# FFN up projection of a decoder trunk: x's hi and x's lo stored side by side and multiplied by the weights' hi in one matmul of 512 columns, with eight PSUM banks as one pool in the FFNs

## The chip, the cores and the metric

The kernel runs on one core of a Trainium2 chip. The metric is the device time of one execution in microseconds (us); smaller is better.

## The reference

Two post-norm layers on an input of 256 tokens by 2048 channels, all in float32. Each layer is a mixer and a feed-forward network (FFN) with a short causal convolution, each with a residual and a layer norm (LN). The part that the change touches is the FFN:

```python
D_MODEL = 2048; SEQ = 256; DEPTH = 2; D_FF = 5632; FFN_CONV = 3
# every layer: x <- LN(alpha*x + mixer(x)); x <- LN(alpha*x + conv_ffn(x))
# conv_ffn: u = x @ w_up                     (2048 -> 2*5632: gate half, value half)
#           u = causal depthwise conv of 3 taps over the tokens
#           y = (silu(gate) * value) @ w_down  (5632 -> 2048)
```

## The kernel before

**Three-term products.** Every float32 operand of a large matmul is split into hi (rounded to the type that TensorE multiplies) and lo (the rest). A product is three matmuls that add into one PSUM tile: hi·hi, hi·lo and lo·hi. Weights come as 1 MB blocks of 512 rows by 512 columns (`load_w`: DMA into `raw`, ACT makes `hi` at L127, DVE makes `lo` at L128). Eight `hi` and eight `lo` buffers let the loads run ahead of TensorE. x lies transposed, channels on partitions, in tiles `XH` (hi) and `XL` (lo), stored as [partition, token half t, channel tile k, 128 tokens]. The 256 tokens of one channel tile are therefore two pieces of 128 with a gap between them.

**Three kinds of projection.** `proj_a` holds weights still and streams the 256 tokens: per channel tile kt and output tile ct it issues L145 (hi·XH), L146 (hi·XL) and L147 (lo·XH), 256 columns each. `proj_b` holds x still and streams 512 weight columns (L178, L179, L181). `proj_halves` does the same for one token half after the other (L213 to L215); the last two column blocks of each output projection run in it, so that the LN of half t=0 can begin while half t=1 is still being multiplied. `proj_bt` is a `proj_b` whose result is transposed afterwards. It makes the first block after an LN, because it can work on half t=0 before half t=1 exists.

**Stages.** `run` goes through even mixer, FFN 0, odd mixer, FFN 1. An FFN has 11 pairs. A pair is a gate block (`proj_bt` in pair 0, `proj_a` in the others) and a value block (`proj_a`), each followed by the convolution (`conv`: ACT L312, DVE L313 and L314 per output tile), and a part of the down projection. During pairs 2 to 9 of FFN 0 a block `s5_prep_block` each is put in, which prepares tables for the odd mixer: eight transposes (L700), eight small matmuls (L709, sixteen instructions in the trace), a DVE copy and a DVE add (L711, L715), and one matmul on their result (L717).

**LN.** `layer_norm(t)`: bn_aggr and L257 on DVE, a power on POOL (L258), four DVE operations L260, four L266, then per column block four transposes on TensorE (L274), an ACT copy to `XH` (L277) and a DVE subtraction to `XL` (L278).

**PSUM.** Eight banks: a pool `acc` of four tiles (one bank each) and a pool `ps` of four, for the whole program. `proj_a` takes two `acc` tiles, `ps` serves transposes and the small matmuls of the stages.

**Order.** The instructions of each engine are put into one fixed order when the program is built, by a scheduler that takes buffers and dependences into account. An engine carries out its instructions in that order, and an instruction that waits holds all that stand behind it on its engine.

Of the kernel before, what the change touches and what calls it, by code (L numbers as in the profile page):

```python
# [7 lines left out]
F32 = mybir.dt.float32  # L8
F32R = mybir.dt.float32r
AF = mybir.ActivationFunctionType  # L10
ALU = mybir.AluOpType
AX = mybir.AxisListType
PSUM = bass.MemoryType.PSUM
DRAM = bass.MemoryType.DRAM

P = 128
T = 256
D = 2048
KT = D // P
DFF = 5632  # L20
# [8 lines left out]
ALL = slice(None)  # L29
# [32 lines left out]
class Build:  # L62
    def __init__(self, ctx, tc, I, O, cols):
        self.tc, self.nc, self.I, self.O = tc, tc.nc, I, O
        self.cols = cols
        nc = self.nc
        self.nld, self.alternate = 0, False
        ctx.enter_context(nc.allow_non_contiguous_dma(reason="strided weight blocks"))
        pool = lambda n, b, **k: ctx.enter_context(tc.tile_pool(name=n, bufs=b, **k))
        self.cp = pool("cp", 1)  # L70
        self.rawp = pool("rawp", 3)
        self.hip = pool("hip", 8)
        self.lop = pool("lop", 8)
        self.sm = pool("sm", 2)
        self.W = self.cp.tile([P, NW, 2, 512], F32, name="W")
        self.accp = pool("accp", 4, space=PSUM)
        self.psp = pool("psp", 4, space=PSUM)
        self.drp = pool("drp", 1, space=DRAM)
        self.Xd = self.drp.tile([T, D], F32, name="Xd")
        self.XHt = [self.cp.tile([P, 2, 8, P], F32R, name=f"XH{k}") for k in range(2)]  # L80
        self.XLt = [self.cp.tile([P, 2, 8, P], F32R, name=f"XL{k}") for k in range(2)]
        ncst = sum(w for _, w in cols[0].values())
        cst = self.cp.tile([P, ncst], F32, name="cst")
        self.cst = cst
        g = lambda n: cst[:, cols[0][n][0]:cols[0][n][0] + cols[0][n][1]]
        self.ident, self.ones = g("ident"), g("ones")
        col = g("col")
        self.eps6, self.one, self.mhalf = (col[:, k:k + 1] for k in range(3))

    def xh(self, t, k, n=None):  # L90
        return self.XHt[k // 8][:, t, k % 8, :] if n is None else self.XHt[k // 8][:, t, k % 8:k % 8 + n, :]

    def xl(self, t, k, n=None):
        return self.XLt[k // 8][:, t, k % 8, :] if n is None else self.XLt[k // 8][:, t, k % 8:k % 8 + n, :]

    def ps(self):
        return self.psp.tile([P, 512], F32, name="ps")

    def acc(self):
        return self.accp.tile([P, 512], F32, name="acc")  # L100
# [30 lines left out]
    def proj_a(self, src, c0, epi, n=512, nkt=KT, pre=None):  # L131
        nc = self.nc
        nct = n // P
        accs = [self.acc() for _ in range((nct + 1) // 2)]
        for kg in range(nkt // 4):
            if pre and kg:
                pre(4 * kg, 4)
            w = self.load_w(src, kg * 512, c0, n, pre=pre if kg == 0 else None)
            for k in range(4):
                kt = kg * 4 + k  # L140
                xh, xl = self.xh(ALL, kt), self.xl(ALL, kt)
                for ct in range(nct):
                    a = accs[ct // 2][:, (ct % 2) * T:(ct % 2) * T + T]
                    wh, wl = (x[:, ct * P:ct * P + P] for x in w(k))
                    nc.tensor.matmul(a, wh, xh, start=kt == 0 and ct % 2 == 0, stop=False, skip_group_check=True)  # L145
                    nc.tensor.matmul(a, wh, xl, start=False, stop=False, skip_group_check=True)  # L146
                    nc.tensor.matmul(a, wl, xh, start=False, stop=kt == nkt - 1, skip_group_check=True)  # L147
        epi(accs)

    def proj_bt(self, src, c0, epi, buf, n=512, skip=0, side=None, tok_outer=True):  # L150
        nc = self.nc
# [148 lines left out]
    def conv_ffn(self, l, final, bg=None):  # L300
        nc, I = self.nc, self.I
        cw = self.wk.tile([P, 88, 3], F32, name="fcw")
        nc.sync.dma_start(cw, I["fcw"][l])
        up, down = I["ffn_w_up"][l], I["ffn_w_down"][l]
        hs = {}

        def conv(accs, ct0, dst):
            for ct in range(4):
                a = accs[ct // 2][:, (ct % 2) * T:(ct % 2) * T + T]
                w = lambda k: cw[:, ct0 + ct, k:k + 1]  # L310
                o = dst[:, ct, :]
                nc.scalar.activation(o, a, AF.Identity, scale=w(2))  # L312
                nc.vector.scalar_tensor_tensor(o[:, 1:], a[:, :T - 1], w(1), o[:, 1:], op0=ALU.mult, op1=ALU.add)  # L313
                nc.vector.scalar_tensor_tensor(o[:, 2:], a[:, :T - 2], w(0), o[:, 2:], op0=ALU.mult, op1=ALU.add)  # L314

        def pair(p):
            gt = self.w4k(4 + p % 2)

            def eg(accs):
                conv(accs, p * 4, gt)  # L320
                nc.scalar.activation(gt, gt, AF.Silu)

            def ev(accs):
                vt = self.w4k(6 + p % 2)
                conv(accs, 44 + p * 4, vt)
                nc.vector.tensor_tensor(vt, vt, gt, op=ALU.mult)
                hh = self.wk.tile([P, 4, T], F32R, name="hh", bufs=2)
                hl = self.wk.tile([P, 4, T], F32R, name="hl", bufs=2)
                nc.scalar.activation(hh, vt, AF.Copy)
                nc.vector.tensor_tensor(hl, vt, hh.bitcast(F32), op=ALU.subtract)  # L330
                hs[p] = (hh, hl)

            if p == 0:
                self.proj_bt(up, 0, eg, self.w4(8))
            else:
                self.proj_a(up, p * 512, eg)
            self.proj_a(up, DFF + p * 512, ev)

        def down_part(ps, last=None):
            lhs = lambda kt, t: tuple(h[:, kt % 4, t * P:t * P + P] for h in hs[ps[kt // 4]])  # L340
            self.out_add(down, ps[0] * 512, 4 * len(ps), lhs, ps[0] == 0, last)

        for p in range(NFF):
            pair(p)
            if bg and p in bg:
                bg[p]()
            if 0 < p < NFF - 1:
                down_part([p - 1])
        self.ln_params(I["ln_ffn_g"], I["ln_ffn_b"], l, (9, 10, 11, 12))
        down_part([NFF - 2, NFF - 1], lambda t: self.layer_norm(t, final, not final))  # L350
# [15 lines left out]
    def even_mixer(self):  # L366
# [91 lines left out]
        for t in range(2):  # L458
            ps = self.ps()
            for j in range(4):  # L460
                nc.tensor.transpose(ps[:, j * P:j * P + P], kd[:, j, t * P:t * P + P], self.ident)
            nc.scalar.copy(kdT[:, t, :], ps)
# [634 lines left out]
                                    op=ALU.subtract)  # L1097
            self.proj_a(self.I["glu_w"], ci * 512, eg, nkt=8)

    def dump(self, name):  # L1100
        nc = self.nc
        for which in ("XH", "XL"):
            n = f"{name}_{which}"
            if n in self.O:
                for k in range(2):
                    nc.sync.dma_start(self.O[n].rearrange("p (t k c) -> p t k c", t=2, k=16)[:, :, 8 * k:8 * k + 8],
                                      getattr(self, which + "t")[k].bitcast(F32))
        if f"{name}_X" in self.O:
            for cc in range(4):
                nc.sync.dma_start(self.O[f"{name}_X"].rearrange("p (t d) -> p t d", t=2)[:, :, cc * 512:cc * 512 + 512], self.X[cc])  # L1110

    def run(self, upto=4):
        nc = self.nc
        self.st = {}
        if upto >= 1:
            with self.phase("wk0", True):
                self.even_mixer()
            self.dump("m0")
        if upto >= 2:
            bg = {1: self.s5_prep_small}  # L1120
            for b in range(8):
                bg[b + 2] = lambda b=b: self.s5_prep_block(b)
            with self.phase("wk1"):
                self.conv_ffn(0, False, bg)
            self.dump("f0")
        if upto >= 3:
            with self.phase("wk2", True):
                self.odd_mixer()
            self.dump("m1")
        if upto >= 4:  # L1130
            with self.phase("wk3"):
                self.conv_ffn(1, True)

    @contextmanager
    def phase(self, name, mixer=False):
        with self.tc.tile_pool(name=name, bufs=1) as wk:
            self.wk = wk
            if mixer:
                self.W2 = wk.tile([P, 4, 2, 512], F32, name="W2")
            yield  # L1140
# [56 lines left out]
```

## Time and profile before

| | |
|---|---|
| median of 3 runs (lowest to highest) | 2462.37 us (2460.4 to 2462.51) |
| profiled execution, its own time | 2460.67 us |
| span in its profile | 2458.8 us, so 1.9 us lie outside |
| TensorE (PE) busy | 2424.9 us, 99% of the span |
| DVE, ACT, POOL busy | 1524.7, 1105.8, 638.8 us |
| granted TensorE clock, mean | 0.991 of full speed (2.4 GHz) |

The profiled execution is 1.7 us below the median of the runs. In the profile, L12 is line 12 of the kernel, PE is TensorE and PEld its weight load. A busy PE is one whose pipeline is not empty: a single row gives the time from a matmul's start to its modelled end (0.28 us for 256 columns), and in a dense stream the next one starts earlier.

### The profile page before, as it was taken

The page shows a single profiled execution, that of the slowest core. Times are in us where ns is not written, and L with a number is a line of the kernel's source. Part 1 is how long each engine was busy: PE and PEld are TensorE (multiplying, and loading weights), DVE is VectorE, ACT ScalarE, POOL GpSimd, SP SyncE. Part 2 cuts the span into 40 slices and gives each one's busy share as a digit, 9 for nine tenths or more (in the row PEclk, how much of TensorE's full clock was granted, in tenths as well). Part 3 has the DMA queues.
Part 4 walks back from the last instruction along what each step waited for, and adds up shares of the span by engine and source line. Part 5 has one row for each costly group of instructions (what it writes and reads, how often), then busy time and mean ns, then how long its engine had stood idle before and what let it go on. Part 6 is the DMA issues. An engine that isn't in the chain of part 4 may idle for free.

```text
span 2458.8 us, 41423 instructions
## 1 busy us (share of the span) xinstructions
PE 2424.9 (99%) x16858; PEld 2243.2 (91%) x16858; DVE 1524.7 (62%) x2186; ACT 1105.8 (45%) x1508; POOL 638.8 (26%) x1135
## 2 busy tenths in 40 slices
PE   9999999999999999999999999999999999999998
PEld 8998987999999999999898999987999999999996
DVE  5654567766655566665759155637766666666666
ACT  5634543544444344444344345543644444444442
POOL 0000003614667887720034443620000000000000
PEclk9999999999999999999999899999999999999999
DMA  7645554465565556665684643445655555555552
GB/s 250 208 159 188 186 187 167 165 214 190 176 216 186 175 180 225 224 224 188 196 285 136 182 129 127 161 159 174 222 185 184 184 187 188 187 190 188 185 183 96
DMA packets 269518, 457.17 MB, mean 186 GB/s; under 512 B 32384, under 2 KB 62464, under 8 KB 269328
## 3 DMA queue, kind: packets, MB, share of 16 engines
q1 hardware_dynamic: 269056, 454.40, 55.5%
q8 instruction: 132, 2.16, 0.4%
q14 instruction: 58, 0.48, 0.1%
q10 hardware_dynamic: 272, 0.13, 0.0%
HBM read 438.76 MB, written 15.73 MB: 185 GB/s over the span
## 4 chain that ended last, share of the span: by engine, by line
PE 91%; DVE 5%; DMA 2%; POOL 1%; issue 1%; SPq 0%; ACT 0%; DVEq 0%; POOLq 0%
PE acc L147 17%; PE acc L146 17%; PE acc L145 17%; PE acc L181 10%; PE acc L178 10%; PE acc L179 10%; PE ps L915 2%; DVE lo L128 1%; PE acc L213 1%; PE acc L214 1%; PE acc L215 1%; DMA W<-VTd 1%; PE ps L1058 1%; PE ps L1055 1%; PE ps L709 1%
## 5 line engine op out<-in xcount | busy, mean ns | idle before, releaser
L128 DVE TENSOR_TENSOR lo<-raw,hi 128x1024 fp32r<-128x1024 f32 (+2 forms) x802 | 916.6, 1155 | 755.5 <-ACT hi L127 732.2
L127 ACT ACTIVATE hi<-raw 128x1024 fp32r<-128x1024 f32 (+2 forms) x894 | 827.1, 944 | 1043.7 <-PE acc L146 504.4
L145 PE MATMUL acc<-XH,hi 128*128 128x256 f32 x3808 | 1075.2, 283 | 4.5 <-ACT hi L127 4.5
L147 PE MATMUL acc<-XH,lo 128*128 128x256 f32 x3808 | 1075.6, 283 | 0.4 <-DVE lo L128 0.4
L146 PE MATMUL acc<-XL,hi 128*128 128x256 f32 x3808 | 1075.0, 282 | 0.0
L145 PEld LDWEIGHTS acc<-XH,hi 128*128 128x128 f32 x3808 | 720.6, 189 | 7.7 <-ACT hi L127 4.9
L146 PEld LDWEIGHTS acc<-XL,hi 128*128 128x128 f32 x3808 | 720.8, 189 | 3.3 <-issue 1.9
L147 PEld LDWEIGHTS acc<-XH,lo 128*128 128x128 f32 x3808 | 720.4, 189 | 3.0 <-issue 1.9
L179 PE MATMUL acc<-lo,hh 128*128 128x512 f32 x640 | 253.1, 395 | 0.0
L178 PE MATMUL acc<-hi,hh 128*128 128x512 f32 x640 | 252.1, 398 | 0.0
L181 PE MATMUL acc<-hi,hl 128*128 128x512 f32 x640 | 252.0, 395 | 0.0
L258 POOL TENSOR_TENSOR rs<-rs,cst 128x1 f32<-128x1 f32 x8 | 7.8, 979 | 914.0 <-DVE rs L257 914.0
L179 PE MATMUL acc<-lo,XH 128*128 128x512 f32 (+2 forms) x488 | 185.0, 379 | 1.7 <-DVE lo L128 1.6
L178 PE MATMUL acc<-hi,XH 128*128 128x512 f32 (+2 forms) x488 | 184.8, 380 | 1.0 <-ACT XH L277 1.0
L181 PE MATMUL acc<-hi,XL 128*128 128x512 f32 (+2 forms) x488 | 168.5, 376 | 0.0
L128 POOL TENSOR_TENSOR lo<-raw,hi 128x512 fp32r<-128x512 f32 x92 | 121.2, 1339 | 158.4 <-ACT hi L127 120.1
L181 PEld LDWEIGHTS acc<-hi,hl 128*128 128x128 f32 x640 | 120.2, 188 | 29.2
L178 PEld LDWEIGHTS acc<-hi,hh 128*128 128x128 f32 x640 | 120.3, 188 | 28.4
L179 PEld LDWEIGHTS acc<-lo,hh 128*128 128x128 f32 x640 | 120.3, 188 | 27.6
L226 DVE TENSOR_TENSOR W<-W,acc 128x512 f32<-128x512 f32 x160 | 103.7, 678 | 21.3 <-PE acc L215 21.2
L179 PEld LDWEIGHTS acc<-lo,XH 128*128 128x128 f32 x488 | 92.1, 189 | 19.7 <-DVE lo L128 3.4
L178 PEld LDWEIGHTS acc<-hi,XH 128*128 128x128 f32 x488 | 92.1, 189 | 17.9 <-ACT XH L277 2.0
(338 smaller groups left out, 2209.0 us busy)
## 6 DMA issues: line engine op xcount, KB each, us to landing
raw<-in_ffn_w_up_dram SPq DMA_DIRECT2D x176, 1024.0 KB, 4.9
raw<-in_ffn_w_down_dram SPq DMA_DIRECT2D x88, 1024.0 KB, 5.2
raw<-in_even_w_in_dram SPq DMA_DIRECT2D x43, 1024.0 KB, 5.1
raw<-in_odd_w_in_dram SPq DMA_DIRECT2D x36, 1024.0 KB, 5.0
raw<-in_even_w_out_dram SPq DMA_DIRECT2D x16, 1024.0 KB, 5.1
raw<-in_odd_w_out_dram SPq DMA_DIRECT2D x16, 1024.0 KB, 5.1
CAd<-W SPq DMA_DIRECT2D x16, 256.0 KB, 4.5
VTd<-W SPq DMA_DIRECT2D x8, 512.0 KB, 6.5
```

The source lines that it names most:

```text
L127: nc.scalar.activation(hi[:, k], r, AF.Copy)
L128: (lo_eng or nc.vector).tensor_tensor(lo[:, k], r, hi[:, k].bitcast(F32), op=ALU.subtract)
L145: nc.tensor.matmul(a, wh, xh, start=kt == 0 and ct % 2 == 0, stop=False, skip_group_check=True)
L146: nc.tensor.matmul(a, wh, xl, start=False, stop=False, skip_group_check=True)
L147: nc.tensor.matmul(a, wl, xh, start=False, stop=kt == nkt - 1, skip_group_check=True)
L178: nc.tensor.matmul(a, xh, wh, start=kt == 0, stop=False)
L179: nc.tensor.matmul(a, xh, wl, start=False, stop=False)
L181: nc.tensor.matmul(a, xl, wh, start=False, stop=kt == nkt - 1)
L213: nc.tensor.matmul(a, xh, wh, start=k == 0, stop=False)
L214: nc.tensor.matmul(a, xh, wl, start=False, stop=False)
L226: nc.vector.tensor_tensor(z, z, a, op=ALU.add)
L915: mms = lambda p, w, x: [nc.tensor.matmul(p[:, u * P:u * P + P], w[:, u, :], x[:, u, :], start=True, stop=True) for u in range(4)]
```

## The change

x's hi and lo get one tile `XX` per eight channel tiles, stored as [partition, channel tile, hi or lo, token half, 128 tokens]. For one channel tile the 256 tokens of hi are now one piece, with the 256 tokens of lo right behind. The new `proj_m` multiplies the weights' hi by these 512 columns at once (L168 of the changed kernel) and the weights' lo by the 256 columns of hi (L169). Each output tile takes a whole PSUM bank, so that a block takes four; within a group of four channel tiles it does output tiles 0 and 1 for all four, then 2 and 3. At the end an ACT copy (L172) and a DVE add (L173) join the two halves of each bank. `proj_m` takes the place of `proj_a` in the FFNs: 21 blocks in each FFN, 42 in all. The mixers keep `proj_a`, reading x from the new tile.

The PSUM pools are opened per stage now: four `acc` and four `ps` in a mixer, as before, and one pool of eight `acc` tiles in an FFN, from which `ps` tiles come too. A debugging function `dump`, which did nothing here, is gone.

```diff
-        self.accp = pool("accp", 4, space=PSUM)
-        self.psp = pool("psp", 4, space=PSUM)
...
-        self.XHt = [self.cp.tile([P, 2, 8, P], F32R, name=f"XH{k}") for k in range(2)]
-        self.XLt = [self.cp.tile([P, 2, 8, P], F32R, name=f"XL{k}") for k in range(2)]
+        self.XXt = [self.cp.tile([P, 8, 2, 2, P], F32R, name=f"XX{k}") for k in range(2)]
...
+    def xhl(self, k):
+        return self.XXt[k // 8][:, k % 8].rearrange("p h t c -> p (h t c)")
...
+    def proj_m(self, src, c0, epi, buf):
+
+        nc = self.nc
+        accs = [self.acc() for _ in range(4)]
+        for kg in range(KT // 4):
+            w = self.load_w(src, kg * 512, c0, 512)
+            for h in range(2):
+                for k in range(4):
+                    kt = kg * 4 + k
+                    for ct in (2 * h, 2 * h + 1):
+                        wh, wl = (x[:, ct * P:ct * P + P] for x in w(k))
+                        nc.tensor.matmul(accs[ct], wh, self.xhl(kt), start=kt == 0, stop=False, skip_group_check=True)
+                        nc.tensor.matmul(accs[ct][:, :T], wl, self.xh(ALL, kt), start=False, stop=kt == KT - 1,
+                                         skip_group_check=True)
+        for ct, a in enumerate(accs):
+            nc.scalar.copy(buf[:, ct, :], a[:, T:])
+            nc.vector.tensor_tensor(a[:, :T], a[:, :T], buf[:, ct, :], op=ALU.add)
+        epi([a[:, :T] for a in accs])
...
             else:
-                self.proj_a(up, p * 512, eg)
-            self.proj_a(up, DFF + p * 512, ev)
+                self.proj_m(up, p * 512, eg, self.w4k(8))
+            self.proj_m(up, DFF + p * 512, ev, self.w4k(13))
...
-        with self.tc.tile_pool(name=name, bufs=1) as wk:
-            self.wk = wk
+        with ExitStack() as ctx:
+            pool = lambda n, b, **k: ctx.enter_context(self.tc.tile_pool(name=name + n, bufs=b, **k))
+            wk = self.wk = pool("", 1)
+            self.accp = pool("a", 4 if mixer else 8, space=PSUM)
+            self.psp = pool("p", 4, space=PSUM) if mixer else None
```

The scheduler orders the instructions anew, and three places come out differently beyond the new matmuls. Line numbers of the changed kernel are higher: its L204, L205, L207 are `proj_b` (before L178, L179, L181), L239 to L241 `proj_halves` (L213 to L215), L300 the LN's transposes (L274), L304 its subtraction (L278), L726, L735, L743 the `s5_prep_block` (L700, L709, L717).

**Place 1: TensorE, from a mixer into an FFN** (shown from the odd mixer into FFN 1; the entry into FFN 0 is the same). Before, after the last matmul of `proj_halves`:

```order
L215 MATMUL acc<-hi,XL_82 128x512
L274 MATMUL ps<-cst,W 128x128 x8
L178 MATMUL acc<-hi,XH_80 128x512
L179 MATMUL acc<-lo,XH_80 128x512
...
L274 MATMUL ps<-cst,W 128x128 x4
...
L181 MATMUL acc<-hi,XL_82 128x512 x8
L181 MATMUL acc<-hi,XL_83 128x512 x8
L274 MATMUL ps<-cst,W 128x128 x8
```

In the changed kernel:

```order
L241 MATMUL acc<-hi,XX_74 128x512
L300 MATMUL ps<-cst,W 128x128 x32
L204 MATMUL acc<-hi,XX_74 128x512
L205 MATMUL acc<-lo,XX_74 128x512
L204 MATMUL acc<-hi,XX_74 128x512
```

Before, the transposes of half t=0 (8, 4 and 4) are mixed with `proj_bt`'s matmuls of t=0, 48 of these run, and then the transposes of t=1 follow. Now all 32 transposes of both halves come first, and only then the first matmul of `proj_bt`. That matmul also waits for DVE there: for the last L304 of half t=1, which reads the last `ps` bank of the mixer's pools, whose place the FFN's pool takes over.

**Place 2: TensorE, from FFN 0 into the odd mixer.** Before, at the end of `proj_halves` of FFN 0:

```order
L215 MATMUL acc<-hi,hl 128x512
L274 MATMUL ps<-cst,W 128x128 x16
L178 MATMUL acc<-hi,XH_80 128x512
...
L181 MATMUL acc<-hi,XL_83 128x512 x8
L274 MATMUL ps<-cst,W 128x128 x16
L178 MATMUL acc<-hi,XH_80 128x512
```

In the changed kernel (the 16 transposes stand twice, each after 48 matmuls of `proj_halves`; the rows shown are both places):

```order
L241 MATMUL acc<-hi,hl 128x512
L300 MATMUL acc<-cst,W 128x128 x16
L239 MATMUL acc<-hi,hh 128x512
...
L241 MATMUL acc<-hi,hl 128x512
L300 MATMUL acc<-cst,W 128x128 x16
L204 MATMUL acc<-hi,XX_74 128x512
L205 MATMUL acc<-lo,XX_74 128x512
```

Before, the transposes of t=0 stand behind all 96 matmuls of the two halves, and those of t=1 behind 48 matmuls of the next projection. Now the transposes of t=0 stand between the two halves of `proj_halves`, and those of t=1 directly behind the second half. The next L204 waits for DVE (the last L304 of t=1) here too.

**Place 3: TensorE, a block `s5_prep_block` in FFN 0**, behind the last matmul of a value block and ahead of the down projection. Before:

```order
L147 MATMUL acc<-XH_81,lo 128x256
L700 MATMUL ps<-cst,W 128x128 x8
L709 MATMUL ps<-s_bd,W 128x32 x8
L178 MATMUL acc<-hi,hh 128x512
L179 MATMUL acc<-lo,hh 128x512
...
L717 MATMUL ps<-cst,s_gt 128x128
L178 MATMUL acc<-hi,hh 128x512
```

In the changed kernel:

```order
L169 MATMUL acc<-XX_75,lo 128x256
L726 MATMUL acc<-cst,W 128x128 x8
L735 MATMUL acc<-s_bd,W 128x32 x8
L743 MATMUL acc<-cst,s_gt 128x128
L204 MATMUL acc<-hi,hh 128x512
```

Before, 24 matmuls of the down projection stand between L709 and L717, which needs what DVE makes of L709's result. Now L743 stands directly behind L735. Its input is made by L737 and L741 on DVE, which stand there behind a weight split (L135), the add L173 of the value block's last output tile and, ahead of L741, a convolution step L338 that needs an ACT result.

## Rows read from the trace of the kernel before

**Rows 1.** The page, part 1: busy time of each engine (share of span).
```profile
PE 2424.9 (99%) x16858; PEld 2243.2 (91%) x16858; DVE 1524.7 (62%) x2186; ACT 1105.8 (45%) x1508; POOL 638.8 (26%) x1135
```

**Rows 2.** The page, part 5: ACT's weight copies; busy, mean ns, idle before and releaser.
```profile
L127 ACT ACTIVATE hi<-raw 128x1024 fp32r<-128x1024 f32 (+2 forms) x894 | 827.1, 944 | 1043.7 <-PE acc L146 504.4
```

**Rows 3.** Timeline of PE, steady stretches: start us, duration, instruction.
```profile
1815.31 0.28 PE L145 MATMUL acc<-XH,hi 128*128 128x256 f32 x1
...
1860.74 0.40 PE L178 MATMUL acc<-hi,hh 128*128 128x512 f32 x1
...
1883.15 0.28 PE L145 MATMUL acc<-XH,hi 128*128 128x256 f32 x1
...
95.81 0.28 PE L178 MATMUL acc<-hi,XH 128*128 128x256 f32 x1
...
106.54 0.28 PE L181 MATMUL acc<-hi,XL 128*128 128x256 f32 x1
```

**Rows 4.** Groups of instructions by form: busy us, mean ns, idle before.
```profile
L312 ACT ACTIVATE W<-acc,fcw 128x256 f32<-128x256 f32 x168 | 75.0, 465 | 51.1 <-PE acc L147 37.5 <-DVE W L314 13.7
...
L298 DVE TENSOR_TENSOR XL<-W,XH 128x256 fp32r<-128x256 f32 x20 | 8.3, 420 | 1.9 <-ACT XH L297 1.9
```

**Rows 5.** Timeline, even mixer into FFN 0.
```profile
415.27 0.40 PE L215 MATMUL acc<-hi,XL 128*128 128x512 f32 x1
...
416.79 0.50 PE L178 MATMUL acc<-hi,XH 128*128 128x512 f32 x1 [0.25 <-ACT XH L277]
...
431.13 2.91 DVE L266 SCALAR_TENSOR_TENSOR W<-W,rs 128x512 f32<-128x512 f32 x4
...
432.07 1.33 PE L274 MATMUL ps<-cst,W 128*128 128x128 f32 x8 [1.54 <-DVE W L266]
...
447.56 0.28 PE L145 MATMUL acc<-XH,hi 128*128 128x256 f32 x1
```

**Rows 6.** Timeline, FFN 0 into the odd mixer.
```profile
1182.13 0.40 PE L215 MATMUL acc<-hi,hl 128*128 128x512 f32 x1
...
1182.37 0.40 PE L213 MATMUL acc<-hi,hh 128*128 128x512 f32 x1
...
1184.38 2.73 DVE L260 SCALAR_TENSOR_TENSOR W<-W,mv 128x512 f32<-128x512 f32 x4
...
1190.76 1.41 DVE L266 SCALAR_TENSOR_TENSOR W<-W,rs 128x512 f32<-128x512 f32 x2
...
1193.33 0.39 PE L215 MATMUL acc<-hi,hl 128*128 128x512 f32 x1
...
1210.08 0.47 PE L178 MATMUL acc<-hi,XH 128*128 128x512 f32 x1
```

**Rows 7.** Timeline, odd mixer into FFN 1.
```profile
1697.66 0.50 PE L178 MATMUL acc<-hi,XH 128*128 128x512 f32 x1 [0.76 <-ACT XH L277]
...
1703.38 2.48 DVE L278 TENSOR_TENSOR XL<-ps,XH 128x512 fp32r<-128x512 f32 x4
...
1709.51 2.73 DVE L266 SCALAR_TENSOR_TENSOR W<-W,rs 128x512 f32<-128x512 f32 x4
...
1724.31 0.28 PE L145 MATMUL acc<-XH,hi 128*128 128x256 f32 x1
```

**Rows 8.** Timeline, one of the eight blocks `s5_prep_block` in FFN 0.
```profile
655.44 1.87 PE L709 MATMUL ps<-s_bd,W 128*128 128x32 f32 x16
...
657.14 0.48 PE L178 MATMUL acc<-hi,hh 128*128 128x512 f32 x1
...
657.79 0.28 DVE L711 COPY s_gt<-ps 128x128 f32<-128x128 f32 x1
...
658.77 0.29 DVE L715 TENSOR_TENSOR s_gt<-s_gt,s_dm 16x128 f32<-16x128 f32 x1
```

**Rows 9.** Windows of PE: us, PE busy (count), granted clock (1.00 is 2.4 GHz).
```profile
433.60:437.00 3.40, 3.40 (x11) 0.51 0.00 0
```

**Rows 10.** Windows of PE, in the odd mixer, behind a longer idle time.
```profile
1332.00:1338.00 6.00, 6.00 (x29) 0.50 0.51 170
```

More of the change, by code (lines that the diff above doesn't have):

```diff
@@ L88, in __init__, with xp @@
         self.eps6, self.one, self.mhalf = (col[:, k:k + 1] for k in range(3))
+    def xp(self, hl, t, k, n):
+        x = self.XXt[k // 8]
+        if n is None:
+            return x[:, k % 8, hl, t, :]
+        x = x[:, k % 8:k % 8 + n, hl, t, :]
+        return x if t != ALL else x.rearrange("p k t c -> p t k c")
     def xh(self, t, k, n=None):
-        return self.XHt[k // 8][:, t, k % 8, :] if n is None else self.XHt[k // 8][:, t, k % 8:k % 8 + n, :]
+        return self.xp(0, t, k, n)
     def xl(self, t, k, n=None):
-        return self.XLt[k // 8][:, t, k % 8, :] if n is None else self.XLt[k // 8][:, t, k % 8:k % 8 + n, :]
+        return self.xp(1, t, k, n)
+    def xhl(self, k):
+        return self.XXt[k // 8][:, k % 8].rearrange("p h t c -> p (h t c)")
     def ps(self):
-        return self.psp.tile([P, 512], F32, name="ps")
+        return self.psp.tile([P, 512], F32, name="ps") if self.psp else self.acc()
     def acc(self):
@@ L307, in conv @@
         def conv(accs, ct0, dst):
-            for ct in range(4):
-                a = accs[ct // 2][:, (ct % 2) * T:(ct % 2) * T + T]
+            for ct, a in enumerate(accs):
                 w = lambda k: cw[:, ct0 + ct, k:k + 1]
@@ L333, in pair @@
             if p == 0:
-                self.proj_bt(up, 0, eg, self.w4(8))
-            else:
-                self.proj_a(up, p * 512, eg)
-            self.proj_a(up, DFF + p * 512, ev)
+                self.proj_bt(up, 0, lambda accs: eg([accs[ct // 2][:, ct % 2 * T:ct % 2 * T + T] for ct in range(4)]),
+                             self.w4(8))
+            else:
+                self.proj_m(up, p * 512, eg, self.w4k(8))
+            self.proj_m(up, DFF + p * 512, ev, self.w4k(13))
         def down_part(ps, last=None):
@@ L1098, in s5_glu @@
             self.proj_a(self.I["glu_w"], ci * 512, eg, nkt=8)
[L1100 to L1110, printed above, removed]
     def run(self, upto=4):
@@ L1117, in run @@
                 self.even_mixer()
-            self.dump("m0")
         if upto >= 2:
@@ L1124, in run @@
                 self.conv_ffn(0, False, bg)
-            self.dump("f0")
         if upto >= 3:
@@ L1128, in run @@
                 self.odd_mixer()
-            self.dump("m1")
         if upto >= 4:
```

## The prediction

> **What bounds the kernel now.** I read the busy times first: TensorE is busy 99% of the span, and no other engine over 62% [rows 1]. So the time is the sum of what TensorE issues, at the rate at which it issues it, plus the few places where it waits. Next came the groups of the weight copies: ACT is idle for over 1000 us ahead of L127, mostly until TensorE gives a buffer back [rows 2]. The weights are there before TensorE wants them; loads, ACT and DVE have slack in the steady stretches. Then the timeline: in steady stretches it gives TensorE's real rate (the distance between starts, not the duration in a row), and at the stage boundaries what it waits for: DVE's and ACT's work in the LN.
>
> **Steady rate.** 1. Two `proj_a` blocks of an FFN are 384 matmuls of 256 columns, and take 1860.74 − 1815.31 = 45.43 us: 118.3 ns each. The 96 matmuls of 512 columns behind them take 1883.15 − 1860.74 = 22.41 us: 233.4 ns each. A `proj_b` with 256 columns in one piece takes 10.73 us from its first to its 93rd start: 116.6 ns each [rows 3]. One (kt, ct) step cost 3 × 118.3 = 354.9 ns; it will be 233.4 + 116.6 = 350.0 ns. 42 blocks × 16 kt × 4 ct = 2688 steps × 4.9 ns = **−13 us**. I take the rate of the down projection for the wide matmul, since it is the same shape on the same engine at the same clock. Bounds: 0, if the new operands keep the old rate, and −13.
>
> The Trainium skill (TensorE: Matmul & The Clock Gate, Back-to-back issue gap) gives N/2.4 + 2.5 ns for a gap at full clock; by that, an estimate, a step would go from 327.5 to 325.0 ns and the change would save 6.7 us where the rows give 13. The rows are 7 to 8% above that formula in both shapes, so the rows decide.
>
> 2. The mixers' 3360 `proj_a` matmuls (11424 in all less 42 × 192) read x in one piece of 256 now. At 118.3 − 116.6 = 1.7 ns each that is **−6 us**; nothing, if the gap in x is not what costs the 1.7 ns.
>
> 3. The new epilogue is four ACT copies (0.47 us each, taken from the convolution's L312, which reads the same shape from PSUM) and four DVE adds (0.42 us, from L298) per block [rows 4]: 1.9 and 1.7 us on engines with 55% and 38% of their time free. In FFNs a pair lasts about 68 us (45.4 + 22.4). The next block has four other banks of the eight, and the down projection takes banks whose convolution is long over, except in the pairs with an `s5_prep_block` (6). **0**; uncovered it would cost up to 42 × 1.9 us, for which the banks would have to run out.
>
> **Boundaries.** The order of the changed kernel puts work of TensorE that covered the LN behind the LN.
>
> 4. Into FFN 0 (place 1). Before, TensorE started `proj_bt` for t=0 at 416.79, 1.5 us after its last `proj_halves` matmul, and worked on it while DVE normalized t=1; it waited 1.54 us ahead of the transposes of t=1, and reached the first `proj_a` matmul at 447.56 [rows 5]. Now all 96 matmuls of `proj_bt` stand behind the transposes of t=1 and DVE's last L304. DVE's chain is hardly altered: its last L266 ends at 431.13 + 2.91 = 434.04, the four L304 take 2.48 us [rows 7], and some small operations that share the queue about 0.8 us, my estimate: 437.3. Then 96 × 0.233 = 22.4 us, with 0.3 us for the start: 460.0. The delay is **+12.4 us**.
>
> 5. Into FFN 1 it is the same: L266 ends at 1712.24, four L304 to 1714.72, 0.2 us for the release, 22.4 us to 1737.3, against 1724.31 [rows 7]: **+13.0 us**. Out of FFN 0 (place 2) both halves are exposed. Half t=0: `proj_halves` ends it at about 1182.4, and DVE starts L260 2.25 us after the start of the last matmul (1184.38 against 1182.13). With L260 and L266 of 2.73 us each back to back the LN values are ready at 1189.84 (before, weight splits stood between, until 1192.17). TensorE used to go on at 1182.37 and now does so at about 1190.3, 7.9 us later; the 48 matmuls of t=1 then have their last start at 1193.33 − 1182.37 + 1190.3 = 1201.3. Half t=1: 2.25 + 2.73 + 2.73 and 2.48 for the four L304 makes 1211.5, and 0.2 us for the release. Then 48 matmuls of `proj_bt` for t=0 (11.2 us) to 1222.9, where before t=1 began at 1210.08 [rows 6, 7]: **+12.8 us**. If L204 waits for the ACT copies alone, each of the three is 2.5 us less.
>
> 6. In `s5_prep_block` (place 3), DVE began L711 at 657.79, 0.5 us after L709's end at 657.31, and L715 ended at 659.06, so that 1.75 us passed from L709 to what the last matmul needs; TensorE was at the down projection from 657.14 on [rows 8]. Now nothing stands between, and TensorE waits. Counting DVE's queue from the end of the value block (an ACT weight copy, L172, L135 of 1.2 us, L173, L737, L338, L741), I get 4.3 us, against 2.9 us that TensorE needs for L726 and L735: 1.4 us. Bounds: 0.6 us, if copy and add go through at once, and 3 us, if the two `L727` copies and the convolution hold both queues. Eight blocks: **+11 us** (5 to 24).
>
> 7. The clock. After the 1.54 us wait in [rows 5] the granted clock was 0.51 for 3.4 us, the lower of its two levels (1.2 of 2.4 GHz), so 1.7 us were lost [rows 9]; behind a longer idle time it stood at 0.50 for 6 us, 3 us lost [rows 10]. Four exposed LN waits (one, two, one) of 5 to 20 us will each leave it there on resumption: 4 × 2.4 = **+10 us** (7 to 12). The wait of point 6 is about as long as the 1.54 us one. I take half of the eight: 4 × 1.7 = **+7 us** (0 to 14).
>
> **Sum.** −13 − 6 + 12.4 + 13.0 + 12.8 + 11 + 10 + 7 = +47 us on the profiled execution's own 2460.7: **2508 us**. The median of the runs shown is 1.7 us higher than that execution, well inside what I can tell.
>
> **The rivals.**
> A. *Cheap waits*: L204 does not wait for L304 (−7.5), the small blocks cost 0.6 us (−6) and leave the clock alone (−7), waits at the LN lose 1.7 us each (−3): +24, **2484 us**. For it: DVE is free half the time. Against: the wait on DVE stands in the order. 13%.
> B. *Dear small blocks*: 3 us each and the clock falls in all eight (+13 + 7): **2528 us**. For it: ACT's queue there holds a weight copy, two L172 and two L727 ahead of the convolution. 15%.
> C. *The wide matmul gains nothing*, since 256 + 256 columns cost what 512 do: the change doesn't do what it says. Without the −13 and −6, **2527 us**. Against: the rates in [rows 3]. 8%.
> D. *Faster*: a 512-column matmul here costs much less than two of 256. It decides from (47 + 13)/2688 = 22 ns a step more, that is at 211 ns or less where the down projection took 233.4; at 200 ns it would be 2508 − 2688 × 0.033 = **2418 us**. Against it: all 96 of [rows 3], on the same array at full clock. 5%. The Trainium skill speaks for it: the same section gives about 131 ns per 512-column matmul as a sustained rate; no stretch of this trace shows that.
> E. *The clock oscillates in the FFNs*, because two banks alternate: half clock in a tenth of the FFN stretches, which are 42 × 22.7 us, would lose 48 us: **2556 us**. Against: `proj_a` alternates two banks too, and in its stretches the clock is full, with a mean of 0.991 for the whole. 2%. The Trainium skill (same page, A second HAM failure mode: psum-queue depth-cycling) describes it for 512-column matmuls that change banks.
>
> **How the numbers follow.** My forecast, +30 to +62, has 57%. The range has to reach A on one side and B and C on the other: 2480 to 2538 us leaves out D, E and the far ends. Within 0.2% (4.9 us) is what a measurement of this kernel can't tell from no change. Only D, and a part of A in which the boundaries too come out cheap, go there or below: faster 0.06, same 0.02, slower 0.92.
>
> **What would show it.** In the changed kernel's timeline: starts 350 ns apart per step in `proj_m` (right) or 355 (C); at 415 and 1696 us TensorE doing 32 transposes with gaps of some 20 us, no L204 before the last L304; two gaps of 8 and 10 us at the end of FFN 0; eight gaps of about 1.4 us ahead of L743; a granted clock near 0.5 behind each large gap. I am wrong if L204 starts with half t=0 of the LN, if something else fills the gaps, or if `proj_m`'s steps are 330 ns or less.

## The result and the profile after

The changed kernel takes 2532.23 us (median of 4 runs, 2528.11 to 2537.67) against 2462.44 us before: a ratio of 1.0286, 95% interval 1.0262 to 1.0310. It is slower, as forecast, and inside the range, though 24 us above the predicted 2508. The difference of 69.8 us lies above the forecast's own +30 to +62; the range holds it because it was drawn to reach two rivals. The profiled execution took 2528.11 us with a span of 2526.3, so the difference that the two traces have to explain is 2526.3 − 2458.8 = 67.5 us.

The page of the changed kernel, part 1:

```profile
PE 2436.5 (96%) x14170; PEld 2129.7 (84%) x14170; DVE 1581.7 (63%) x2354; ACT 1167.0 (46%) x1676; POOL 614.1 (24%) x1135
```

TensorE was busy 99% of the span in [rows 1] and is busy 96% now, of a longer span. What it waited for, by the view of the waits (engine, waiting line, releaser: us in total, times, longest):

```profile
PE ps L300 <- DVE W L292: 25.0, 2, 13.1
PE acc L743 <- DVE s_gt L741: 16.7, 8, 3.4
PE acc L300 <- DVE W L292: 12.7, 2, 7.3
...
PE acc L204 <- DVE XX L304: 4.5, 3, 1.7
```

The largest waits are the ones named beforehand: L300, the LN's transposes, 37.7 us for DVE's L292 (L266 before); L204 for the last L304; and L743 in all eight small blocks.

The timeline of TensorE at the three boundaries (start us, duration, instruction, idle before and releaser):

```profile
414.93 0.40 PE L241 MATMUL acc<-hi,XX 128*128 128x512 f32 x1
...
431.71 3.65 PE L300 MATMUL ps<-cst,W 128*128 128x128 f32 x16 [13.06 <-DVE W L292]
437.01 0.80 PE L204 MATMUL acc<-hi,XX 128*128 128x512 f32 x1 [1.66 <-DVE XX L304]
...
462.32 1.10 PE L168 MATMUL acc<-XX,hi 128*128 128x512 f32 x4
...
1220.99 0.40 PE L241 MATMUL acc<-hi,hl 128*128 128x512 f32 x1
1226.78 3.65 PE L300 MATMUL acc<-cst,W 128*128 128x128 f32 x16 [5.39 <-DVE W L292]
...
1249.74 3.36 PE L300 MATMUL acc<-cst,W 128*128 128x128 f32 x16 [7.28 <-DVE W L292]
1254.58 0.50 PE L204 MATMUL acc<-hi,XX 128*128 128x512 f32 x1 [1.47 <-DVE XX L304]
...
1265.88 0.40 PE L204 MATMUL acc<-hi,XX 128*128 128x512 f32 x1
...
1750.15 0.40 PE L241 MATMUL acc<-hi,XX 128*128 128x512 f32 x1
...
1764.92 3.46 PE L300 MATMUL ps<-cst,W 128*128 128x128 f32 x16 [11.94 <-DVE W L292]
1769.79 0.50 PE L204 MATMUL acc<-hi,XX 128*128 128x512 f32 x1 [1.41 <-DVE XX L304]
...
1793.62 0.63 PE L168 MATMUL acc<-XX,hi 128*128 128x512 f32 x2
```

And before, the last `proj_halves` matmul ahead of FFN 1:

```profile
1695.63 0.40 PE L215 MATMUL acc<-hi,XL 128*128 128x512 f32 x1
```

The reader is to compare distances, not positions. Into FFN 0, the first matmul of the FFN's `proj_a` stood 447.56 − 415.27 = 32.3 us behind the last one of `proj_halves` [rows 5]; now 462.32 − 414.93 = 47.4: 15.1 us more. Out of FFN 0, from the last matmul of half t=0 to the start of `proj_bt` for t=1, it was 1210.08 − 1182.13 = 27.95 us [rows 6] and is 1265.88 − 1220.99 = 44.89: 16.9 us more. Into FFN 1, it was 1724.31 [rows 7] − 1695.63 = 28.7 us before and is 1793.62 − 1750.15 = 43.5 now: 14.8 us more. Together **46.8 us**.

Next the small blocks. They lie between the start of pair 2 and that of pair 10 of FFN 0; the start of a pair's gate block in the kernel before:

```profile
540.32 0.28 PE L145 MATMUL acc<-XH,hi 128*128 128x256 f32 x1
...
1103.33 0.28 PE L145 MATMUL acc<-XH,hi 128*128 128x256 f32 x1
```

and in the changed kernel, with two pairs of FFN 1, where there are no such blocks, and the first matmul of a down projection:

```profile
552.95 0.40 PE L168 MATMUL acc<-XX,hi 128*128 128x512 f32 x1
...
1142.41 0.40 PE L168 MATMUL acc<-XX,hi 128*128 128x512 f32 x1
...
1884.25 0.40 PE L168 MATMUL acc<-XX,hi 128*128 128x512 f32 x1
...
1929.47 0.40 PE L204 MATMUL acc<-hi,hh 128*128 128x512 f32 x1
...
1951.87 0.40 PE L168 MATMUL acc<-XX,hi 128*128 128x512 f32 x1
```

Eight pairs with blocks went from 563.0 to 589.5 us: **26.5 us** more. Some 2 us of this is work that only moved. Before, the eight transposes of the first block (L700) ran at 521.75 us, ahead of pair 2, with half of its L709; now they stand behind the start of pair 2. With the two pairs ahead (from the first `proj_a` of FFN 0 on) it was 655.8 us before (447.56 to 1103.33) and is 680.1 now (462.32 to 1142.41): 24.3 us more. A pair of FFN 1 went from 67.84 [rows 3] to 67.62 us, and its two blocks from 45.43 to 45.22 us, which is 353.3 ns a step where 350.0 were predicted and 354.9 were measured before. That is all that the wide matmul gives: 1.6 ns a step, 4.3 us over 2688.

### The profile page after: what moved, and what is told of

Same layout as the page of the kernel before. It is cut to its first block, busy times and chain, and to the rows that moved or that the text cites. A ratio compares the mean times of both kernels' runs of the same rounds, so it can differ in the third digit from the quotient of the medians.

```text
span 2526.3 us, 36369 instructions
## 1 busy us (share of the span) xinstructions
PE 2436.5 (96%) x14170; PEld 2129.7 (84%) x14170; DVE 1581.7 (63%) x2354; ACT 1167.0 (46%) x1676; POOL 614.1 (24%) x1135
## 4 chain that ended last, share of the span: by engine, by line
PE 86%; DVE 7%; POOL 3%; DMA 2%; issue 1%; ACT 1%; SPq 1%; DVEq 0%; ACTq 0%; POOLq 0%
PE acc L168 23%; PE acc L169 12%; PE acc L204 10%; PE acc L205 10%; PE acc L207 10%; PE acc L154 4%; PE acc L153 4%; PE acc L152 4%; DVE lo L135 2%; PE ps L941 2%; PE acc L239 1%; PE acc L240 1%; PE acc L241 1%; PE ps L1036 1%; ACT hi L134 1%
## 5 line engine op out<-in xcount | busy, mean ns | idle before, releaser
L135 DVE TENSOR_TENSOR lo<-raw,hi 128x1024 fp32r<-128x1024 f32 (+2 forms) x802 | 916.5, 1154 | 745.3 <-ACT hi L134 739.0
L168 PE MATMUL acc<-XX,hi 128*128 128x512 f32 x2688 | 949.8, 397 | 0.0
L169 PE MATMUL acc<-XX,lo 128*128 128x256 f32 x2688 | 754.9, 281 | 0.0
L168 PEld LDWEIGHTS acc<-XX,hi 128*128 128x128 f32 x2688 | 504.3, 188 | 124.1
L169 PEld LDWEIGHTS acc<-XX,lo 128*128 128x128 f32 x2688 | 506.6, 189 | 1.5
L152 PE MATMUL acc<-XX,hi 128*128 128x256 f32 x1120 | 320.8, 287 | 3.8 <-ACT hi L134 3.8
L154 PE MATMUL acc<-XX,lo 128*128 128x256 f32 x1120 | 321.2, 288 | 0.5 <-DVE lo L135 0.5
L153 PE MATMUL acc<-XX,hi 128*128 128x256 f32 x1120 | 320.8, 287 | 0.0
L204 PE MATMUL acc<-hi,hh 128*128 128x512 f32 x640 | 257.3, 402 | 0.0
L205 PE MATMUL acc<-lo,hh 128*128 128x512 f32 x640 | 256.2, 400 | 0.0
L207 PE MATMUL acc<-hi,hl 128*128 128x512 f32 x640 | 255.2, 400 | 0.0
L152 PEld LDWEIGHTS acc<-XX,hi 128*128 128x128 f32 x1120 | 215.0, 192 | 5.9 <-ACT hi L134 4.0
L154 PEld LDWEIGHTS acc<-XX,lo 128*128 128x128 f32 x1120 | 215.0, 192 | 3.2 <-issue 1.9
L153 PEld LDWEIGHTS acc<-XX,hi 128*128 128x128 f32 x1120 | 215.2, 192 | 2.3 <-issue 1.9
L204 PE MATMUL acc<-hi,XX 128*128 128x512 f32 (+2 forms) x488 | 184.6, 379 | 4.5 <-DVE XX L304 4.5
L205 PE MATMUL acc<-lo,XX 128*128 128x512 f32 (+2 forms) x488 | 184.1, 377 | 0.0
L207 PE MATMUL acc<-hi,XX 128*128 128x512 f32 (+2 forms) x488 | 168.5, 376 | 0.0
L135 POOL TENSOR_TENSOR lo<-raw,hi 128x512 fp32r<-128x512 f32 x92 | 119.7, 1323 | 177.2 <-ACT hi L134 124.2
L207 PEld LDWEIGHTS acc<-hi,hl 128*128 128x128 f32 x640 | 122.1, 191 | 29.8
L204 PEld LDWEIGHTS acc<-hi,hh 128*128 128x128 f32 x640 | 122.4, 191 | 29.4
```

The lines of the kernel that those rows point to most:

```text
L135: (lo_eng or nc.vector).tensor_tensor(lo[:, k], r, hi[:, k].bitcast(F32), op=ALU.subtract)
L168: nc.tensor.matmul(accs[ct], wh, self.xhl(kt), start=kt == 0, stop=False, skip_group_check=True)
L169: nc.tensor.matmul(accs[ct][:, :T], wl, self.xh(ALL, kt), start=False, stop=kt == KT - 1, skip_group_check=True)
L204: nc.tensor.matmul(a, xh, wh, start=kt == 0, stop=False)
L205: nc.tensor.matmul(a, xh, wl, start=False, stop=False)
L207: nc.tensor.matmul(a, xl, wh, start=False, stop=kt == nkt - 1)
```

## The experiments

Times are medians; ratios are against runs of the kernel before on the same chip (2462.10, 2461.57 and 2462.91 us in the three sessions).

**1. The pools alone.** The kernel before, with the changed kernel's PSUM pools:

```diff
-        self.accp = pool("accp", 4, space=PSUM)
-        self.psp = pool("psp", 4, space=PSUM)
...
+            self.accp = pool("a", 4 if mixer else 8, space=PSUM)
+            self.psp = pool("p", 4, space=PSUM) if mixer else None
```

> The kernel before, with only the PSUM pools of the change: opened per stage, one pool of eight in an FFN. The matmuls, the layout of x and the epilogue are those of before. Theory (the pools cost the time: they put TensorE's work behind the LN at the three boundaries and the last matmul of the small blocks ahead of the down projection): the three boundaries cost 46 to 47 us as in the changed kernel, the eight small blocks 8 to 28 us (their DVE queue is lighter without the new copies and adds), about 2515 to 2537 us. Rival (the wide matmul with its banks and its epilogue costs the time): within 5 us of 2462.

2534.24 us, ratio 1.0289 (1.0270 to 1.0308). The whole loss is there without the wide matmul. The waits of TensorE in this run (its L272 is the LN's transpose, L715 the last matmul of a small block, L176 `proj_bt`'s first):

```profile
PE ps L272 <- DVE W L264: 25.0, 2, 13.1
PE acc L715 <- DVE s_gt L713: 16.3, 8, 3.2
PE acc L272 <- DVE W L264: 12.7, 2, 7.4
...
PE acc L176 <- DVE XL L276: 4.5, 3, 1.6
```

They are those of the changed kernel to within 0.4 us. The rival that the new epilogue, with its copies and adds on ACT and DVE, makes the small blocks dear falls too: 16.3 us without it, 16.7 with it.

**2. The wide matmul with the old pools.** The changed kernel, pools of four and four for the whole program:

```diff
-        accs = [self.acc() for _ in range(4)]
+        accs = [self.ps(), self.ps(), self.acc(), self.acc()]
```

> The changed kernel with the PSUM pools of before (four acc and four ps for the whole program); a block of the wide projection takes two tiles of each, ps for the first two output tiles. Theory (pools): the order at the three boundaries is as before, so what remains is the gain of the wide matmul and of the layout, 4.6 and 1.6 us by the changed kernel's trace: about 2456 us, 2450 to 2460. Rival (wide matmul with its epilogue costs the time): 2500 or more. Second rival (both together): about 2480.

2480.99 us, ratio 1.0078 (1.0061 to 1.0094): neither 2456 nor 2500. The boundaries are as before, and FFN 1 gains. But FFN 0 is longer by 7 us (from its first wide matmul, 447.08, to pair 10, 1109.87: 662.8 us against 655.8 before), and the stretch from the first `proj_a` of the odd mixer to FFN 1 by 15.5 (1240.50 to 1746.01). The largest waits of TensorE in this run that the kernel before has not, or has much shorter:

```profile
PE ps L1083 <- DMA W<-Gd: 5.1, 2, 4.5
PE ps L737 <- ACT hi L136: 5.0, 3, 2.0
```

L737 is in the small blocks; they need `ps` banks, of which the wide projection now holds two. That this is what it waits for is argued: the row names ACT's weight copy. L1083, and with shorter waits L1038 (2.8 us) and L943 (1.9 us), are in the odd mixer, whose code and pools are untouched but for the layout of x. TensorE's order there is new. Why the scheduler sets it otherwise stays open; that TensorE waits there is shown. That the order costs all of the 15.5 us is not shown: experiment 10 loses 9.8 us in this mixer in the order of before.

**3. The layout alone.** Old pools, three matmuls of 256 columns, x in the new tile.

```diff
-                self.proj_m(up, p * 512, eg, self.w4k(8))
-            self.proj_m(up, DFF + p * 512, ev, self.w4k(13))
+                self.proj_a(up, p * 512, lambda accs: eg(halves(accs)))
+            self.proj_a(up, DFF + p * 512, lambda accs: ev(halves(accs)))
```

> The kernel before, with only the new layout of x (hi and lo side by side), three matmuls of 256 columns and the old pools. Theory: the mixers gained 1.6 us over 3360 matmuls, 0.5 ns each; for all 11424 it would be 5 us: about 2457 us. If the 1.7 ns that the prediction took is right, 19 us less: 2443 us. If the layout is worth nothing: 2462 us.

2460.06 us, ratio 0.9987 (0.9976 to 0.9997): 2 us or so, not 19. The timeline shows why, two blocks of an FFN and the down projection behind them:

```profile
1882.41 0.28 PE L154 MATMUL acc<-XX,hi 128*128 128x256 f32 x1
...
1927.86 0.40 PE L206 MATMUL acc<-hi,hh 128*128 128x512 f32 x1
```

384 matmuls in 45.45 us are 118.4 ns each. It was 118.3 with the gap in x [rows 3]. The layout is worth nothing per matmul; where the 2 us of the total come from is open.

**4. All four banks of a wide block from the pool of four.** As 2, with `accs = [self.acc() for _ in range(4)]` kept.

> The changed kernel with the old pools, and all four tiles of a block of the wide projection from the acc pool of four. Theory: the order at the boundaries is as before, but each block waits for the convolution of the block ahead of it, since it needs the same four banks: 2 to 4 us for each of 42 blocks, and half the clock behind some of them: 2540 to 2640 us. Rival (a block needs no second set of four banks): about 2456 us.

2516.01 us, ratio 1.0215 (1.0197 to 1.0233). It is 54 us above before, less than the expected 80 and more, and the theory fails in FFN 1, which has no small blocks. Two blocks there (timeline):

```profile
1868.86 0.40 PE L170 MATMUL acc<-XX,hi 128*128 128x512 f32 x1
...
1914.06 0.39 PE L206 MATMUL acc<-hi,hh 128*128 128x512 f32 x1
```

45.20 us for 128 steps are 353.1 ns a step, as in the changed kernel, and no block of FFN 1 waits for a bank. There the rival is right: four banks are enough. The loss lies in FFN 0 and behind it: the first `proj_a` of the odd mixer starts 46.1 us later than before (1280.34 against 1234.29), and from there to FFN 1 it takes 7.4 us more (497.4 against 490.0), while FFN 1 is 1.5 us shorter. In FFN 0 the new order puts the first part of the small blocks between the gate and the value block. The longest waits are one of 7.0 us of the wide projection for the residual add of a down projection, five of together 7.3 us for the convolution, as the theory has it, and seven of 16.5 us of the small blocks for POOL.

**5. The tail of the small blocks behind the down projection.** The changed kernel, with L743 and what follows it issued after `down_part`:

```diff
         nc.vector.tensor_tensor(gT[:16], gT[:16], dm, op=ALU.add)
+        yield
         ps = self.ps()
...
-                bg[p]()
+            rest = bg[p]() if bg and p in bg else None
+            if rest:
+                next(rest)
             if 0 < p < NFF - 1:
                 down_part([p - 1])
+            if rest:
+                next(rest, None)
```

> The changed kernel, with the last matmul of each small block (L743, its ACT copy and its store) put behind the down projection, with its input still made where it was. Theory: the eight waits ahead of L743 (16.7 us in the changed kernel's trace) and the half clock behind them go away, while the three boundaries stay: 28 us less than the changed kernel, about 2504 us. Rival (the wait moves to the first matmul of the down projection, whose bank the value block's convolution has to free): 2520 to 2532 us.

2510.92 us, 21 us below the changed kernel, ratio to before 1.0192 (1.0169 to 1.0215). The wait for L741 is gone, and the waits at the boundaries stand:

```profile
PE ps L300 <- DVE W L292: 25.0, 2, 13.1
PE acc L300 <- DVE W L292: 13.1, 2, 7.7
```

Its eight pairs take 564.7 us (from 551.83 to 1116.53), 24.8 less than in the changed kernel and 1.7 more than before. The wait did not move to the down projection, so that rival falls. Of the 24.8 us the odd mixer took back 6.7: from its first `proj_a` to FFN 1 it takes 510.3 us, in the changed kernel 503.6. TensorE's order there is the same in both.

**6. Wide, wide, narrow, narrow.** The changed kernel, another order of four matmuls:

```diff
-                        wh, wl = (x[:, ct * P:ct * P + P] for x in w(k))
+                        wh = w(k)[0][:, ct * P:ct * P + P]
                         nc.tensor.matmul(accs[ct], wh, self.xhl(kt), start=kt == 0, stop=False, skip_group_check=True)
+                    for ct in (2 * h, 2 * h + 1):
+                        wl = w(k)[1][:, ct * P:ct * P + P]
                         nc.tensor.matmul(accs[ct][:, :T], wl, self.xh(ALL, kt), start=False, stop=kt == KT - 1,
```

> The changed kernel, with the four matmuls of two output tiles in another order: wide, wide, narrow, narrow in place of wide, narrow, wide, narrow. Question: why a step of the wide projection takes 353.3 ns and not the 350.0 that were predicted. Theory (the pair costs what its columns cost and 1 to 2 ns for each matmul that follows one of another width): fewer changes of width, 351 to 352 ns, 2528 us. Rival (the rate is that of the columns, whatever the order): 353 ns and 2532 us.

2529.91 us, ratio 1.0270 (1.0250 to 1.0291), not to be told from the changed kernel's by its total; the rate can be:

```profile
1960.11 0.63 PE L168 MATMUL acc<-XX,hi 128*128 128x512 f32 x2
...
2005.06 0.40 PE L206 MATMUL acc<-hi,hh 128*128 128x512 f32 x1
```

128 steps in 44.95 us, 351.2 ns each, against 353.3. This order of widths is worth 2 ns a step.

**7. The wide projection in FFN 1 alone.** As 2, with `proj_a` in FFN 0 (`if l:` around `proj_m`).

> Old pools for the whole program, the new layout, the wide projection in FFN 1 alone (two ps and two acc tiles a block), FFN 0 with three matmuls of 256 columns. In the run with the wide projection in both FFNs and these pools, FFN 1 was 2 us shorter than before, while FFN 0 and the odd mixer were longer. Theory (the losses there come from the new order and the banks in FFN 0): 2456 to 2460 us. Rival (FFN 1's gain is eaten by another order elsewhere): 2462 or more.

2461.52 us, ratio 0.9992 (0.9979 to 1.0005): no difference. From the first `proj_a` of the odd mixer to FFN 1 it takes 6.8 us longer than before in the profiled execution (496.8 against 490.0), more than FFN 1 gains; TensorE's waits there include 2.5 us for Gd (1.5 before) and 2.1 us for Ud (0.7 before). The rival named another order as the reason; TensorE's order there is that of before, so this is not shown. Experiment 9, with the same pools and the same order in this mixer, takes 491.0 us.

**8. Pools per stage, but four and four.** Experiment 1 without the pool of eight:

```diff
-            self.accp = pool("a", 4 if mixer else 8, space=PSUM)
-            self.psp = pool("p", 4, space=PSUM) if mixer else None
+            self.accp = pool("a", 4, space=PSUM)
+            self.psp = pool("p", 4, space=PSUM)
```

> The kernel before with PSUM pools opened per stage, but of four and four in the FFNs too. Theory (it is the one pool of eight that takes the place of both old pools and so puts all transposes of the LN ahead, not the opening per stage): the order at the boundaries and in the small blocks stays nearly as before, 2462 us, at most 5 us more. Rival (the opening of a new pool makes the next stage wait): the two entries into the FFNs cost 15 us each, 2490 us or more.

2479.29 us, ratio 1.0058 (1.0038 to 1.0078): between the two. The entry into FFN 0 and the stretch out of FFN 0 cost about 1 us each where the pool of eight cost 15 to 17, and FFN 0's pairs 0.7. TensorE does the transposes of t=0, then `proj_bt` for t=0, then the transposes of t=1. So far the theory holds: it is the pool of eight that sets all 32 transposes ahead and L743 behind L735. From the first `proj_a` of the odd mixer to FFN 1 it loses 15.8 us (505.8 against 490.0): 10.9 up to the last `proj_halves` matmul and 4.9 at the entry into FFN 1. From the end of FFN 0 to FFN 1 its largest wait that the kernel before has not:

```profile
PE acc L176 <- DVE W L224: 6.6, 2, 4.0
```

L176 is the first matmul behind an LN, held for 4.0 us at the entry into FFN 1 and for the rest at that into the odd mixer, so opening a pool per stage is not free either.

**9 and 10. Eight wide, then eight narrow matmuls**, in FFN 1 alone (as 7) and in both FFNs (as 2): the loop over k stands once around the wide and once around the narrow ones.

> As the run with the wide projection in FFN 1 alone (old pools, new layout), with eight wide matmuls of a group and then its eight narrow ones. Two wide and two narrow brought a step from 353.7 to 351.7 ns. Theory (each change of width costs): 350 ns a step, a pair of FFN 1 in 67.2 us against 67.85 before, so 6 to 7 us less in FFN 1 than before; the odd mixer was 7 us longer in the other run by its new order, which may go either way: 2450 to 2462 us. Rival (two and two was all there is): 351.7 ns and 2455 to 2465 us.

> The same with the wide projection in both FFNs: old pools, two ps and two acc tiles a block, eight wide and then eight narrow matmuls. The run without that order took 2481 us, 5 us longer in FFN 0 and 15 us longer in the odd mixer than before. Theory: 2688 steps at 3.7 ns less, 10 us less than that run, 2466 to 2476 us. Rival (the order of steps is worth nothing): 2481 us.

2463.53 us, ratio 1.0007 (0.9997 to 1.0017), and 2484.32 us, ratio 1.0080 (1.0068 to 1.0093). No gain over 7 and 2 in the total. A pair of FFN 1 in 9 takes 1953.30 − 1885.35 = 67.95 us, more than the changed kernel's 67.62; in these pairs TensorE waits 0.3 us for ACT's weight copy amid the wide matmuls (nine times, 2.6 us). Without such a break, two blocks of FFN 0 in 10 (256 matmuls from 608.07 to 653.09) take 351.7 ns a step: less than 353.3, but no less than the 351.2 of experiment 6. My theory that fewer changes of width keep helping falls, and the rival (two and two was all there is) stands; what does decide between 351 and 353 ns is open. In 10 the small blocks wait 10.7 us for the convolution, five times, and the odd mixer is 9.8 us longer than before.

No version beats the kernel before by more than the 0.1% of experiment 3.

## Why the prediction was right, point by point

**Direction and mechanism: right, and shown.** The boundaries and the small blocks were named as the loss; the waits there are the ones forecast, and the pools alone bring them (experiment 1 for the sum, 5 for the blocks, 8 for the eight in one). In FFN 1 the wide projection itself costs nothing and gains little. The parts do not add up, though: with the old pools (2) the kernel loses 19 us in other places.

**The size: in part luck.** +47 us was predicted, +69.8 measured, outside the +30 to +62 that had 57%. It lies close to rivals B (2528) and C (2527), and each of them came true in part. Inside the sum, errors of one sign in points 1, 2 and 6 add up, and two in the boundaries cancel.

**Points 4 and 5 with their share of 7, the boundaries: right.** 38.2 us of delay and 10 of clock were predicted, 46.8 measured. L204 starts at 437.01, predicted 437.3. The two terms are off against each other, and that they cancel is luck: about 4 us of the 46.8 are clock, so some 42.6 are delay. `proj_bt` takes 25.3 us into FFN 0 and 23.8 into FFN 1, not 22.4, partly because its own transposes wait for ACT (0.68 us at 450.62). And the clock cost less. Windows of PE in the changed kernel (us, busy, granted clock):

```profile
435.50:437.00 1.50, 0.00 (x0) 0.50 0.00 0
...
437.00:443.00 6.00, 5.99 (x19) 0.73 0.00 0
...
1227.00:1233.00 6.00, 6.00 (x25) 0.57 0.53 178
...
1253.20:1254.60 1.40, 0.03 (x1) 1.00 0.87 220
1254.60:1260.60 6.00, 6.00 (x26) 1.00 0.84 245
1769.80:1775.80 6.00, 6.00 (x26) 1.00 0.12 46
```

TensorE resumed at the lower level, 0.50, each time, as predicted. But at two of the four exposures the clock is full again when `proj_bt` starts: about 1.6 and 2.6 us are lost in the windows at 437.00 and 1227.00, none in those at 1254.60 and 1769.80. Three of the four resume alike, with 16 transposes and then the wait for L304. Behind 1249.74 and 1764.92 the clock had risen before that wait was over; behind 431.71 it stayed at 0.50 through the transposes and the wait, into `proj_bt`. What decides between them is open.

**Point 6 with its share of 7, the small blocks: mis-sized.** 11 us of waits and 7 of clock were predicted; the waits are 16.7 and the pairs lose 24.3 us in all, with the gain of the wide matmul in it. The step that failed is "1.4 us": it holds in some blocks and not in others. A dear block and a cheap one (timeline):

```profile
665.34 3.69 DVE L135 TENSOR_TENSOR lo<-raw,hi 128x1024 fp32r<-128x1024 f32 x3
...
668.94 0.76 DVE L173 TENSOR_TENSOR acc<-acc,W 128x256 f32<-128x256 f32 x2
...
669.85 0.28 PE L169 MATMUL acc<-XX,lo 128*128 128x256 f32 x1
...
675.11 0.27 DVE L741 TENSOR_TENSOR s_gt<-s_gt,s_dm 16x128 f32<-16x128 f32 x1
...
675.52 0.30 PE L743 MATMUL acc<-cst,s_gt 128*128 128x128 f32 x1 [2.81 <-DVE s_gt L741]
...
742.31 0.79 DVE L173 TENSOR_TENSOR acc<-acc,W 128x256 f32<-128x256 f32 x2 [0.56 <-ACT W L172]
...
744.77 0.28 PE L169 MATMUL acc<-XX,lo 128*128 128x256 f32 x1
...
748.39 0.27 DVE L741 TENSOR_TENSOR s_gt<-s_gt,s_dm 16x128 f32<-16x128 f32 x1
...
748.81 0.30 PE L743 MATMUL acc<-cst,s_gt 128*128 128x128 f32 x1 [1.18 <-DVE s_gt L741]
```

In the first DVE does its first L173 0.9 us before the value block's last matmul starts, in the second 2.5 us before, and L741 ends late by as much. In the first DVE comes from three weight splits L135 in a row, behind an ACT copy that waited 0.46 us for a DMA; I took one L135 between the value block and L737, where two stand in both, and did not ask where DVE's queue stood. The clock behind each of them (windows):

```profile
675.50:679.50 4.00, 3.98 (x11) 0.57 0.91 302
748.80:752.80 4.00, 3.99 (x18) 1.00 0.99 330
```

Behind the dear wait the clock was at its lower level for most of 4 us, behind the cheap one it was full. By the windows behind all eight it was low five times, 0.50 to 0.68, behind waits of 1.55 to 3.40 us, and full three times, behind waits of 1.18 to 1.24 us; four of eight were predicted. That is rival B in part, two of its three us a block.

**Point 1, the wide matmul: mis-sized.** −13 us was predicted, −4.3 is what the pairs of FFN 1 give for 2688 steps. The step that failed is the rate of the down projection (233.4 and 116.6 ns) for matmuls of two widths by turns: together they take 353.3, not 350.0. Experiment 6 brings it to 351.2. Part of the miss is the 116.6: experiment 3 has 118.4 ns for 256 columns of an FFN in one piece, and 233.4 + 118.4 would be 351.8, an estimate. The change nearly does what rival C said, 1.6 ns a step from no gain at all. (Rival D's bound counts the 13 us twice: the sum of +47 is gone at 47/2688 = 17.5 ns a step, that is at 216 ns and not at 211. Nothing hangs on it here.)

By the formula of the Trainium skill (TensorE: Matmul & The Clock Gate, Back-to-back issue gap) the saving would be 2.5 ns a step, an estimate; measured are 1.6. The Trainium skill's sustained 131 ns for 512 columns, rival D, is nowhere in these runs.

**Point 2, the mixers: wrong, and small.** −6 us predicted for reading x in one piece; experiment 3 shows the same 118 ns with and without the gap. The 1.7 ns against the 256-column `proj_b` has another cause, which is open. The condition that I had put on the lower bound, "if the gap in x is not what costs the 1.7 ns", is what holds.

**Point 3, the epilogue: right.** Pairs of FFN 1 are no longer than their matmuls, and no wait of TensorE for L172 or L173 is among the largest.

**The sum.** Predicted −13 − 6 + 48 + 18 = +47. Measured: +46.8 at the boundaries, +26.5 in the eight pairs, −2.1 in the first pairs of FFN 0 (from +14.8 us at 462.32 to +12.6 at 552.95; mostly the work that moved), −1.6 in the two mixers, −1.8 from the start of FFN 1 to the end, and −0.2 in the rest of FFN 0: +67.6. The wide matmul's −4.3 is spread over the terms of the FFNs. Of the 20 us that the forecast lacked, about 8 are the small blocks', which cost more than predicted, and about 9 and 4 are gains of the wide matmul and of the layout that did not come; the boundaries came out 1 us cheaper.

## What to carry to other kernels

A pool of PSUM banks is part of the schedule. One pool of eight in place of two of four, opened per stage, put the layer norm's transposes and the work behind them into another order and cost 70 us, while the matmul for which it was done gained 4. It did not even need the pool: in FFN 1 it ran at the same rate with four banks (experiment 4). Compare the order of each engine at the seams between stages, and price what TensorE can no longer do under a vector chain. And before the layout is rebuilt, time the wide matmul in its own order with its neighbours: 512 columns at once take nearly the time of twice 256.

## What the runs showed that I had not expected

A stage whose code is unchanged can lose 10 us and more. From its first `proj_a` to its last `proj_halves` matmul the odd mixer takes 461.3 us before, 476.8 in experiment 2 and 472.2 in 8; in these two TensorE's order there is another. But it also takes 466.8 us in 5, 468.1 in 7 and 471.2 in 10, where the 3264 matmuls ahead of `proj_halves` stand in the order of before. The stretch in the kernel before and in 10 (us, busy, granted clock):

```profile
1234.29:1695.63 461.34, 448.70 (x3337) 0.97 0.52 166
...
1249.18:1720.34 471.16, 458.54 (x3338) 0.95 0.52 163
```

The mean granted clock is lower in 5, 7 and 10 (0.95) than before and in the changed kernel (0.97). So these three losses are not the order of TensorE's work, and how much of the 15.5 us in 2 is, these runs don't show. A change that is meant to gain 4 us is below this.

What a granted clock at the lower level costs depends on when it rises again: at 1254.58 and at 1769.79 it was full when `proj_bt` began, at 437.01 it was not, behind the same 16 transposes.
